# Decay scans ahead of the last attention head, the MLP norm applied to the second product's sums, a 384/128 cut of the last token tile: one change to a one-core decoder block

## The chip, the cores and the metric

The kernel runs on one core of one Trainium2 chip, as one launch. The metric is the device time of one execution in microseconds (us); the time before is the median of 3 runs. Five engines work side by side, each through its own queue in order: TensorE (PE in the profile, with PEld for its weight loads), VectorE (DVE), ScalarE (ACT), GpSimd (POOL) and SyncE (SP). PE reads SBUF and writes PSUM banks of 128 x 512 float32; DVE and ACT read both; transfers are issued from the queues of SP, ACT and POOL.

## What is computed

One layer of a decoder on 512 tokens of width 1024, all float32. Only what the change touches is shown in full:

```
h   = rmsnorm(x, ln1);  one projection h @ w_in -> GLA q,k,v,r,a | attention q,k,v (3 groups) | 2 gates
o   = gla_mixer(q, k, v, log_sigmoid(a @ w_a2 + b_a) / 16)      # 4 heads, chunks, cumulative decay
oat = dilated attention, 3 groups x 4 heads, merged by their softmax denominators
x   = x + (sigmoid(gA) * (o' @ w_o_gla) + sigmoid(gB) * (oat @ w_o_attn)) @ w_out
h2  = rmsnorm(x, ln2)
x   = x + square(relu(h2 @ w_mlp1)) @ w_mlp2
h3  = rmsnorm(x, ln3)
x   = x + sigmoid(h3 @ w_pg) * (p @ w_pp)
out = rmsnorm(x, ln_f)
```

The norm of a token is one factor r = (mean of squares + eps) ** -0.5. Since r is positive, square(relu(r * z)) is r * r * square(relu(z)), so the factor can be put on the hidden units before the square, or, squared, on the sums of the second product.

## The kernel before

**Products.** Every float32 operand is split into a rounded high part and the rest (hi, lo), and a product is three matmuls (hi hi, hi lo, lo hi). `run` (L234 to L241) writes the matmuls to PE in pieces of 8 and calls `step` after each piece; all of them stand on line L240. Most 1024-wide products are done as quads (`strassen`, L266): a 2 x 2 block scheme with 7 stages of 24 matmuls of 256 columns instead of 8 block products. A bank that is finished is copied out by ACT (L312) and the other half added by DVE (L330, L332).

**Weights.** Units of 128 x 1024 stream in through SP (L189). For quads POOL issues transfers that add a second block onto one that has landed (L198, L209), and DVE makes the remaining sums (L206, L212). ACT makes hi (L226), DVE makes lo (L221), a few units ahead of their use (`fetch`, L215).

**What sets the order.** The order is written out by hand. Beside the products stand generators in a list `side`, and closures in a list `later`. `step` (L168) runs one closure of `later` and, once `pace[0]` columns have been written since, one segment of the first generators of `side`, in turn by two (WAYS = 2). `drain` runs all that is left, with no product between.

**Around the change, in the order of the program.** After the attention's v0 the four heads' weighted sums `pv(h)` (scaled probabilities, transposes on PE at L769, products at L775 to L786, a sum on DVE at L788, split at L337 and L345) and then `decay()` are put into `side`, at a pace of 2560 columns, beside the quads gq, gk and gv0. `decay` makes, for each GLA head, a product (L801), an absolute value and a minimum (L805, L806), an exponential (L811), a logarithm (L814) and a cumulative sum by a scan on DVE (L817, L818). After a `drain` come the products `oa` (L1002: 8 tiles of 12 matmuls of 512 columns) with `gla(0)` and `gla(1)` beside them, whose first segments read the cumulative sums (L836 to L861) and are followed by transposes on PE (L869).

Behind w_out the MLP's first product runs as 8 quads (`quad(q)`, L1158 on). Its norm is made by `rms_gen` beside it: four one-column products (L377), the factor by DVE and POOL (L364, L365), a diagonal matrix (L390), its split, and two products that spread the factor over all partitions (L396, L397). Each finished bank is multiplied by it (`scale`, L1167) and squared by ACT (L1176). After the first quad there is a `drain` if the norm isn't there. The second product (L1200 on) sums over 32 hidden units into 4 banks, twice; DVE adds the banks to x (L1226) and `normed` prepares the last norm's operand (L339, L347, L1089).

At the end the gate product `pg` runs per tile of 128 tokens. Per tile: a sigmoid (L1267), a product (L1268), an addition (L1269), a square with a row sum (L1270), the factor (L1281, L1282), then the two halves of the output (L1284, L1290) and their transfers (L1285 on ACT's queue, L1292 on SP's). The last tile's second half is cut into two times 256 columns.

Of the kernel before, what the change touches and what calls it, by code (L numbers as in the profile page):

```python
# [13 lines left out]
AF = mybir.ActivationFunctionType  # L14
# [112 lines left out]
C_LN2, C_LN3, C_BA, C_GN, C_LN1, C_LO, C_N = 0, 8, 16, 20, 28, 36, 38  # L127
W0, W12 = 384, 256

NU, NW, PIECE, WAYS = 69, 5, 8, 2  # L130

NRAW = 6

NWARM = 8

# [2 lines left out]
def block_kernel(ctx, tc, xT, ws, pT, wts, wha, wa2, vec, lnf, rel, onehot, ident_d, mask_d, out):  # L138
# [141 lines left out]
    def halves(t):  # L280
        return slice(t * HT, (t + 1) * HT)
# [88 lines left out]
        S.activation(t, x, AF.Square, scale=1.0 / 32.0)  # L370
        return t

    def rms_tok(acc):

        ps = smt()
        for i in range(4):
            TE.matmul(ps[:, i:i + 1], lhsT=acc[:, i * P:(i + 1) * P], rhs=ones[:, 0:1], start=True, stop=True)  # L377
        r = const.tile([P, 4], F32, name="rtok", bufs=3)
        rsqrt(r, ps[:, 0:4], 4)
        return r  # L380

    def rms_gen(acc, res, wait=0, gap=0):

        for _ in range(wait):
            yield
        r = rms_tok(acc[0])
        for _ in range(gap):
            yield
        dg = u32()
        V.tensor_tensor(dg.rearrange("p (a b) -> p a b", a=4), ident[:, None, :].to_broadcast([P, 4, P]),  # L390
                        r[:, :, None].to_broadcast([P, 4, P]), op=OP.mult)
        dh, dl = split(dg)
        for _ in range(2 + gap):
# [593 lines left out]
    side.append(weights())  # L987
    v0 = values("v0")
    drain()
    pace[0] = 2560  # L990
    side.extend(pv(h) for h in range(4))
    side.append(decay())
    gq = heads("gq", HD_SCALE)
    gk = heads("gk", 1.0)
    gv = [values("gv0", True)]
# [152 lines left out]
        later.extend(x1_tile(j))  # L1148
    while len(later) > 5:
        step()  # L1150
    side.append(rms_gen(acc1, norm2, 6, 2))


    hid = [None] * 32
# [4 lines left out]
    def quad(q):  # L1159


        def finish(m, t, s, ps):
            add(m, s, s, ps)

            def scale():
                o = s.rearrange("p (n t) -> p n t", n=2)
                V.scalar_tensor_tensor(out=o, in0=o, scalar=0.0,  # L1167
                                       in1=norm2[1][:, None, halves(t)].to_broadcast([P, 2, HT]),
                                       op0=OP.max, op1=OP.mult)

            def act():
                for n in range(2):
                    j = 4 * q + 2 * n + m
                    if hid[j] is None:
                        hid[j] = u32()
                    S.activation(hid[j][:, halves(t)], s[:, halves(n)], AF.Square)  # L1176

            later.extend([scale, act])

        def extra(i):  # L1180
            if i in (3, 4):
                later.append(lambda: hid_split(i - 3))

        strassen(f"m1q{q}", x1_op, finish, extra=extra if q == 7 else None)
# [6 lines left out]

    for q in range(8):
        quad(q)
        if q == 0 and not norm2:
            drain()
    for k in (2, 3):
        hid_split(k)
    drain()
# [2 lines left out]
    for sub in range(2):  # L1201
# [21 lines left out]
                    lnb.append(t)  # L1223
        for o in range(4):
            j = 4 * sub + o
            V.tensor_tensor(xx[j], xx[j], pss[o], op=OP.add)  # L1226
            normed(j, C_LN3, x2s, acc2)
    while later:
        step()
# [30 lines left out]
    sp2 = const.tile([P, 4], F32, name="sp2")  # L1260
    fr = const.tile([P, 4], F32, name="fr")

    def gated(ps, i, c, tt, col):

        n = c.stop - c.start
        sg = u32()
        S.activation(sg[:, 0:n], ps[:, 0:n], AF.Sigmoid, scale=rt3[0][:, tt:tt + 1])  # L1267
        V.tensor_tensor(sg[:, 0:n], sg[:, 0:n], pps[i][:, c], op=OP.mult)  # L1268
        V.tensor_tensor(x2t[i][:, c], x2t[i][:, c], sg[:, 0:n], op=OP.add)  # L1269
        S.activation(sg[:, 0:n], x2t[i][:, c], AF.Square, scale=1.0 / 32.0, accum_out=ss2[:, col:col + 1])  # L1270

    def evac_pg0(tt, ps):
        if len(x2t) < 8:
            drain()
        gated(ps, tt, slice(0, 512), tt, tt)
        V.tensor_scalar(sp2[:, tt:tt + 1], ss2[:, tt:tt + 1], EPS, None, op0=OP.add)
        V.tensor_tensor(x2t[tt], x2t[tt], lnb[0], op=OP.mult)

    def scale_out(tt, col):
# [2 lines left out]
        GP.tensor_tensor(fr[:, tt:tt + 1], sp2[:, tt:tt + 1], mh[:, 0:1], op=OP.pow)  # L1282
        o = u32()
        S.activation(o, x2t[tt], AF.Copy, scale=fr[:, tt:tt + 1])  # L1284
        S.dma_start(out[tt * P:(tt + 1) * P, 0:512], o)  # L1285

    def put(tt, c):
        n = c.stop - c.start
# [3 lines left out]
        SY.dma_start(out[tt * P:(tt + 1) * P, 512 + c.start:512 + c.stop], o[:, 0:n])  # L1292

    def evac_pg1(tt, ps):
        gated(ps, 4 + tt, slice(0, 512), tt, 4 + tt)
        scale_out(tt, 4 + tt)
        put(tt, slice(0, 512))

    tmaj("pg0", x2s, evac_pg0)
    tmaj("pg1", x2s, evac_pg1, tts=range(3))  # L1300
    tok = slice(3 * P, 4 * P)
    for f in range(2):
        c = slice(f * 256, (f + 1) * 256)
# [94 lines left out]
```

## Time and profile before

| | us |
|---|---|
| median of 3 runs | 990.1 (989.91 to 991.78) |
| the profiled execution | 991.5 |
| its span (first to last instruction) | 989.7 |
| PE busy in the span | 973.7 |
| DVE, ACT, POOL busy in the span | 689.4, 520.9, 94.4 |

The profiled execution is 1.8 us longer than its span and 1.4 us above the median. Busy time of PE is the union of overlapping matmuls; a product that streams in a row is read by the distance from start to start, not by its own length.

### The profile page before, as it was taken

What the parts mean: (1) busy time and instruction counts of PE and PEld (TensorE: products, weight loads), DVE (VectorE), ACT (ScalarE), POOL (GpSimd) and SP (SyncE); (2) the same over time, 40 slices, a digit from 0 to 9 for tenths busy, and PEclk for the clock granted to TensorE, in tenths of its full rate; (3) what the DMA queues carried; (4) which work ended last, traced back from release to release, by engine and by line L of the source; (5) the groups of instructions that cost most, each with busy time, mean ns of one, the idle gap of its engine ahead of it and who ended that gap; (6) DMA issues with size and microseconds to landing.
All of it is one profiled execution on the core that took longest, in us unless ns stands there. A gap on an engine that the chain in (4) does not pass through costs nothing.

```text
span 989.7 us, 15873 instructions
## 1 busy us (share of the span) xinstructions
PE 973.7 (98%) x6372; PEld 889.3 (90%) x6372; DVE 689.4 (70%) x966; ACT 520.9 (53%) x875; POOL 94.4 (10%) x136
## 2 busy tenths in 40 slices
PE   9999999999998999999999999999999999999996
PEld 7788999999996999999988889999998888888885
DVE  7777579676579669977955697788778445653554
ACT  7335546445575667565733446555665335442633
POOL 0230011320010021013010001010000000000000
PEclk9999999999999999999999999999999999999999
DMA  8473564974264545455636426656544332523102
GB/s 308 126 205 100 128 147 112 266 202 115 80 157 131 160 98 149 121 146 171 171 92 206 126 46 164 177 131 169 154 145 131 104 96 77 167 88 106 43 1 85
DMA packets 40026, 133.63 MB, mean 135 GB/s; under 512 B 5203, under 2 KB 6815, under 8 KB 39952
## 3 DMA queue, kind: packets, MB, share of 16 engines
q1 hardware_dynamic: 27504, 92.51, 28.5%
q0 software_dynamic: 10720, 36.96, 18.4%
q10 hardware_dynamic: 1728, 3.15, 0.8%
q8 instruction: 50, 0.82, 0.3%
q14 instruction: 24, 0.20, 0.1%
HBM read 126.26 MB, written 8.17 MB: 136 GB/s over the span
## 4 chain that ended last, share of the span: by engine, by line
PE 92%; DVE 3%; issue 2%; ACT 1%; POOL 0%; POOLq 0%; DVEq 0%; ACTq 0%
PE mmt L240 73%; PE smt L240 9%; PE smt L829 1%; DVE lo L221 1%; PE smt L769 1%; PE smt L695 1%; PE mmt L454 1%; PE mmt L453 1%; PE mmt L455 1%; PE smt L875 1%; DVE u L818 0%; PE smt L877 0%; PE smt L428 0%; PE smt L665 0%; PE smt L786 0%
## 5 line engine op out<-in xcount | busy, mean ns | idle before, releaser
L240 PE MATMUL mmt<-ur,hi 128*128 128x256 f32 (+1 forms) x2784 | 608.5, 314 | 1.8 <-ACT u L1002 1.5
L240 PEld LDWEIGHTS mmt<-ur,hi 128*128 128x128 f32 x2784 | 459.9, 191 | 34.3 <-issue 1.9
L240 PE MATMUL mmt<-ur,lo 128*128 128x256 f32 (+1 forms) x1392 | 437.4, 314 | 0.5 <-DVE lo L221 0.5
L221 DVE TENSOR_TENSOR lo<-w,hi 128x1024 fp32r<-128x1024 f32 x236 | 286.2, 1220 | 119.6 <-PE mmt L240 64.2
L226 ACT ACTIVATE hi<-w 128x1024 fp32r<-128x1024 f32 x236 | 246.8, 1053 | 137.1 <-issue 64.0
L240 PEld LDWEIGHTS mmt<-ur,lo 128*128 128x128 f32 x1392 | 266.0, 191 | 16.3 <-DVE lo L221 0.7
L240 PE MATMUL mmt<-hi,ur 128*128 128x256 f32 (+1 forms) x736 | 154.5, 306 | 0.0
L337 ACT ACTIVATE ur<-u 128x512 fp32r<-128x512 f32 x136 | 79.9, 621 | 95.2 <-DVE u L1066 30.9
L240 PEld LDWEIGHTS mmt<-hi,ur 128*128 128x128 f32 x736 | 119.4, 191 | 5.6
L240 PE MATMUL mmt<-lo,ur 128*128 128x256 f32 (+1 forms) x368 | 112.4, 305 | 0.0
L345 DVE TENSOR_TENSOR ur<-u,ur 128x512 fp32r<-128x512 f32 x135 | 89.0, 686 | 20.3 <-ACT ur L337 19.7
L330 DVE TENSOR_TENSOR u<-u,mmt 128x512 f32<-128x512 f32 (+1 forms) x92 | 58.0, 654 | 39.0 <-PE mmt L240 37.4
L240 PE MATMUL smt<-ur,hi 128*128 128x512 f32 x272 | 83.7, 389 | 0.0
L312 ACT ACTIVATE u<-mmt 128x512 f32<-128x512 f32 x92 | 54.4, 592 | 49.7 <-PE mmt L240 49.7
L240 PEld LDWEIGHTS mmt<-lo,ur 128*128 128x128 f32 x368 | 70.2, 191 | 2.7
L240 PEld LDWEIGHTS smt<-ur,hi 128*128 128x128 f32 x272 | 51.1, 188 | 10.6
L240 PE MATMUL smt<-ur,lo 128*128 128x512 f32 x136 | 53.0, 390 | 0.0
L209 POOL DMA_DIRECT2D w<-in_wts_dram x23 | 20.1, 875 | 289.8 <-DVE w L206 210.5
L1176 ACT ACTIVATE u<-u 128x256 f32<-128x256 f32 x64 | 23.0, 409 | 37.2 <-DVE u L1167 37.2
L198 POOL DMA_DIRECT2D w<-in_wts_dram x23 | 20.4, 886 | 202.4 <-DMA w<-in_wts_dram 84.6
L240 PEld LDWEIGHTS smt<-ur,lo 128*128 128x128 f32 x136 | 25.5, 188 | 5.3
L212 DVE TENSOR_TENSOR w<-w 128x1024 f32<-128x1024 f32 x23 | 28.2, 1225 | 0.8
(203 smaller groups left out, 718.2 us busy)
## 6 DMA issues: line engine op xcount, KB each, us to landing
w<-in_wts_dram SPq DMA_DIRECT2D x167, 512.0 KB, 4.0
w<-in_wts_dram POOLq DMA_DIRECT2D x46, 512.0 KB, 5.5
u<-in_xT_dram SPq DMA_DIRECT2D x8, 256.0 KB, 4.7
v_dram<-u POOLq DMA_DIRECT2D x8, 256.0 KB, 6.2
u<-v_dram POOLq DMA_DIRECT2D x8, 256.0 KB, 7.3
y_dram<-u ACTq DMA_DIRECT2D x8, 256.0 KB, 2.4
u<-y_dram POOLq DMA_DIRECT2D x8, 256.0 KB, 7.3
u<-in_xT_dram POOLq DMA_DIRECT2D x8, 256.0 KB, 8.1
```

Of the source, the lines that this page charges most:

```text
L198: GP.dma_start(w, wts[UNIT[f"{q}.A22"]], accum_op=OP.add)
L209: GP.dma_start(w, wts[UNIT[f"{q}.A21"]], accum_op=OP.add)
L212: V.tensor_tensor(w, w, raw[f"{q}.A12"], op=OP.add)
L221: V.tensor_tensor(lo, w, hi.bitcast(F32), op=OP.subtract)
L226: S.activation(hi, w, AF.Copy)
L240: TE.matmul(o, lhsT=l, rhs=r, start=a, stop=b, skip_group_check=shared)
L312: S.activation(sums[c], bank[b], AF.Copy, scale=-scale if c[0] else scale)
L330: V.tensor_tensor(out, s, ps, op=OP.subtract if m else OP.add)
L337: S.activation(hi, x, AF.Copy)
L345: V.tensor_tensor(lo, x, hi.bitcast(F32), op=OP.subtract)
L453: TE.matmul(q0ps[i], lhsT=hi[:, c], rhs=xh, start=k == 0, stop=False)
L1176: S.activation(hid[j][:, halves(t)], s[:, halves(n)], AF.Square)
```

## The change

Five edits. (1) `decay` stands ahead of `pv(3)` in the list, and the pace of that stretch stays at 2048 columns instead of 2560. (2) The MLP's norm is made as the square of the factor, by a reciprocal on DVE instead of a power on POOL, starts 30 steps later (6 before), with gaps of 4 steps (2 before); the hidden units are only clipped at zero, and the factor is applied where the second product's banks are added to x, by one more DVE operation for each of the 8 banks. The `drain` after the first quad is gone. (3) The last tile's second half is cut 384 + 128 columns, and the order of its steps is changed: the second sigmoid stands ahead of the first square. (4) Of the first output halves, those of tiles 0 to 2 leave by SP's queue, that of tile 3 by ACT's. (5) The arena has 73 tiles instead of 69, and the space for the descriptors of POOL's transfers is 8192 bytes of each partition instead of 16384.

```diff
-NU, NW, PIECE, WAYS = 69, 5, 8, 2
+NU, NW, PIECE, WAYS = 73, 5, 8, 2
+LAST = 384
...
-    def rms_tok(acc):
+    def rms_tok(acc, squared=False):
...
-        rsqrt(r, ps[:, 0:4], 4)
+        if squared:
+            V.tensor_scalar(r, ps[:, 0:4], EPS, None, op0=OP.add)
+            V.reciprocal(r, r)
+        else:
+            rsqrt(r, ps[:, 0:4], 4)
...
-    pace[0] = 2560
-    side.extend(pv(h) for h in range(4))
-    side.append(decay())
+    side.extend([pv(0), pv(1), pv(2), decay(), pv(3)])
...
-    side.append(rms_gen(acc1, norm2, 6, 2))
+    side.append(rms_gen(acc1, norm2, 30, 4, True))
...
-            def scale():
-                o = s.rearrange("p (n t) -> p n t", n=2)
-                V.scalar_tensor_tensor(out=o, in0=o, scalar=0.0,
-                                       in1=norm2[1][:, None, halves(t)].to_broadcast([P, 2, HT]),
-                                       op0=OP.max, op1=OP.mult)
+            def positive():
+                V.tensor_scalar(s, s, 0.0, None, op0=OP.max)
...
-        if q == 0 and not norm2:
-            drain()
...
-            V.tensor_tensor(xx[j], xx[j], pss[o], op=OP.add)
+            t = u32()
+            V.tensor_tensor(t, pss[o], norm2[1], op=OP.mult)
+            V.tensor_tensor(xx[j], xx[j], t, op=OP.add)
...
-        S.dma_start(out[tt * P:(tt + 1) * P, 0:512], o)
+        (S if tt == 3 else SY).dma_start(out[tt * P:(tt + 1) * P, 0:512], o)
...
-    for f in range(2):
-        c = slice(f * 256, (f + 1) * 256)
-        ps = mmt()
...
-        gated(ps, 7, c, 3, 8 + f)
-        if f == 0:
-            V.tensor_scalar(sp2[:, 3:4], ss2[:, 8:9], sp2[:, 3:4], None, op0=OP.add)
+    parts, sgs = [slice(0, LAST), slice(LAST, 512)], []
+    for c in parts:
+        ps, n = mmt(), c.stop - c.start
...
+        sgs.append(gate(ps, n, 3))
+        if c.start == 0:
+            gated(sgs[0], 7, c)
+    squares(sgs[0], 7, parts[0], 8)
+    gated(sgs[1], 7, parts[1])
+    V.tensor_scalar(sp2[:, 3:4], ss2[:, 8:9], sp2[:, 3:4], None, op0=OP.add)
+    squares(sgs[1], 7, parts[1], 9)
...
-    nc = _bacc.Bacc("TRN2", target_bir_lowering=False, num_devices=1)
+    nc = _bacc.Bacc("TRN2", target_bir_lowering=False, num_devices=1, dynamic_dma_scratch_size=8192)
```

How the order moves, at three places. (The changed kernel has other line numbers: L817 and L818 of before are L823 and L824, L221 is L223, L330 is L332, L345 is L347. Numbers behind a name are buffers.)

DVE at the end of gv0 and the start of `oa`, before: scans (L817, L818) stand among the last sums of gv0 (L330) and directly ahead of the first segment of `gla` (L837).

```order
L818 SCALAR_TENSOR_TENSOR u_3035<-u_135,u_3036 128x512
L345 TENSOR_TENSOR ur_3276<-u_3182,ur_3264 128x512
L817 TENSOR_TENSOR u_3080<-u_3080,u_3079 128x512
L818 SCALAR_TENSOR_TENSOR u_3079<-u_135,u_3080 128x512
L330 TENSOR_TENSOR u_3109<-u_3109,mmt_3011 128x512
L817 TENSOR_TENSOR u_3112<-u_3112,u_3111 128x512
L818 SCALAR_TENSOR_TENSOR u_3111<-u_135,u_3112 128x512
L330 TENSOR_TENSOR u_3146<-u_3146,mmt_3011 128x512
L345 TENSOR_TENSOR ur_3288<-u_3109,ur_3284 128x512
L345 TENSOR_TENSOR ur_3290<-u_3146,ur_3286 128x512
L221 TENSOR_TENSOR lo_3294<-w_3171,hi_3241 128x1024
L837 TENSOR_TENSOR u_3308<-u_3003 128x4x64
```

The same place now, from the last of the four scans (L824) on; the first segment of `gla` follows two rows behind the piece.

```order
L824 SCALAR_TENSOR_TENSOR u_2860<-u_135,u_2861 128x512
L223 TENSOR_TENSOR lo_3179<-w_2788,hi_3147 128x1024
L223 TENSOR_TENSOR lo_3212<-w_3108,hi_3181 128x1024
L332 TENSOR_TENSOR u_3081<-u_3081,mmt_3185 128x512
L347 TENSOR_TENSOR ur_3245<-u_3081,ur_3235 128x512
L223 TENSOR_TENSOR lo_3247<-w_3149,hi_3214 128x1024
L332 TENSOR_TENSOR u_3194<-u_3194,mmt_3072 128x512
L347 TENSOR_TENSOR ur_3280<-u_3194,ur_3270 128x512
L332 TENSOR_TENSOR u_3119<-u_3119,mmt_3013 128x512
L332 TENSOR_TENSOR u_3159<-u_3159,mmt_3013 128x512
L347 TENSOR_TENSOR ur_3288<-u_3119,ur_3284 128x512
L347 TENSOR_TENSOR ur_3290<-u_3159,ur_3286 128x512
```

What moved: the last scans stood among the last sums of gv0 (L330); now all four stand ahead of the last four of these sums (L332), and between the last scan and `gla` there are only sums, splits and weight parts. On PE the last product of `pv(3)` now stands 144 matmuls of 256 columns ahead of the first matmul of `oa`.

DVE in the MLP's first quads, where the norm's factor is made, before (rv and rtok are the factor, u<-ident,rtok the diagonal matrix, rstd the factor on all partitions):

```order
L345 TENSOR_TENSOR ur_6456<-u_6372,ur_6444 128x512
L221 TENSOR_TENSOR lo_6458<-w_6323,hi_6422 128x1024
L364 TENSOR_SCALAR rv_6481<-smt_6475 128x4
L390 TENSOR_TENSOR u_6500<-ident_116,rtok_6480 128x512
L345 TENSOR_TENSOR ur_6504<-u_6500,ur_6502 128x512
L221 TENSOR_TENSOR lo_6506<-w_5928,hi_6460 128x1024
L221 TENSOR_TENSOR lo_6536<-w_6134,hi_6508 128x1024
L221 TENSOR_TENSOR lo_6577<-w_6462,hi_6538 128x1024
L330 TENSOR_TENSOR u_6434<-u_6434,mmt_6545 128x512
L1167 SCALAR_TENSOR_TENSOR u_6434<-u_6434,rstd_6559 128x512
```

The same work now, a quad later:

```order
L1170 TENSOR_SCALAR u_6503<-u_6503 128x512
L223 TENSOR_TENSOR lo_6696<-w_6597,hi_6661 128x1024
L223 TENSOR_TENSOR lo_6731<-w_6228,hi_6698 128x1024
L382 TENSOR_SCALAR rtok_6750<-smt_6745 128x4
L383 RECIPROCAL rtok_6750<-rtok_6750 128x4
L223 TENSOR_TENSOR lo_6769<-w_6462,hi_6733 128x1024
L396 TENSOR_TENSOR u_6797<-ident_116,rtok_6750 128x512
L347 TENSOR_TENSOR ur_6801<-u_6797,ur_6799 128x512
L223 TENSOR_TENSOR lo_6811<-w_6700,hi_6771 128x1024
L332 TENSOR_TENSOR u_6673<-u_6673,mmt_6778 128x512
L1170 TENSOR_SCALAR u_6673<-u_6673 128x512
```

What moved: factor, matrix and split have weight parts between them, and no longer stand ahead of the first hidden sum. On PE, 48 matmuls stood between the one-column products (L377) and the spreading products (L396) before, 6 of them behind the place of L364; now 80.

ACT's last instructions, before (L1267 sigmoid, L1270 square, L1284 output half):

```order
L1284 ACTIVATE u_10052<-u_9680,fr_9779 128x512
L1285 DMA out_0_dram<-u_10052 128x512
L1267 ACTIVATE u_10083<-mmt_10058,rtok_9733 128x256
L1270 ACTIVATE u_10083,ss2_9777<-u_9815 128x256
L1267 ACTIVATE u_10114<-mmt_10089,rtok_9733 128x256
L1270 ACTIVATE u_10114,ss2_9777<-u_9815 128x256
L1284 ACTIVATE u_10121<-u_9696,fr_9779 128x512
L1285 DMA out_0_dram<-u_10121 128x512
```

And now (L1266 sigmoid, L1277 square, L1296 output half, L1297 its transfer):

```order
L1296 ACTIVATE u_10067<-u_9695,fr_9794 128x512
L1266 ACTIVATE u_10098<-mmt_10073,rtok_9748 128x384
L1266 ACTIVATE u_10127<-mmt_10102,rtok_9748 128x128
L1277 ACTIVATE u_10098,ss2_9792<-u_9830 128x384
L1277 ACTIVATE u_10127,ss2_9792<-u_9830 128x128
L1296 ACTIVATE u_10136<-u_9711,fr_9794 128x512
L1297 DMA out_0_dram<-u_10136 128x512
```

What moved: tile 2's transfer is no longer ahead of the last tile's first sigmoid, and the second sigmoid has passed the first square.

## Rows read from the trace of the kernel before

**Rows 1.** Part 1 of the page: each engine's busy time, its share of the span, its instructions.

```profile
PE 973.7 (98%) x6372; PEld 889.3 (90%) x6372; DVE 689.4 (70%) x966; ACT 520.9 (53%) x875; POOL 94.4 (10%) x136
```

**Rows 2.** What PE waited for, over the whole span: us in total, times, the longest.

```profile
PE smt L869 <- DVE u L857: 2.4, 2, 1.6
PE smt L396 <- ACT ur L337: 1.6, 1, 1.6
PE mmt L240 <- ACT u L1002: 1.5, 1, 1.5
PE mmt L240 <- DVE lo L221: 0.5, 1, 0.5
```

**Rows 3.** PE in order of time in the products `oa` with `gla(0)` and `gla(1)` beside them: start, us, instruction, count, idle time before it and what ended it.

```profile
303.20 0.39 PE L240 MATMUL mmt<-ur,lo 128*128 128x512 f32 x1
...
303.88 0.39 PE L240 MATMUL mmt<-ur,lo 128*128 128x512 f32 x1
304.60 0.70 PE L240 MATMUL mmt<-ur,hi 128*128 128x512 f32 x2 [0.32 <-DVE u L330]
...
312.80 0.55 PE L869 MATMUL smt<-ident,u 128*128 128x128 f32 x3 [1.62 <-DVE u L857]
313.10 0.47 PE L240 MATMUL mmt<-ur,lo 128*128 128x512 f32 x1
...
315.09 0.55 PE L869 MATMUL smt<-ident,u 128*128 128x128 f32 x3 [0.82 <-DVE u L857]
315.39 0.71 PE L240 MATMUL mmt<-ur,hi 128*128 128x512 f32 x2
```

**Rows 4.** DVE in order of time in the same stretch: the first and the last scan, the first operation of `gla`, the last one that the second group of transposes (L869) needs.

```profile
295.92 1.23 DVE L818 TENSOR_TENSOR_SCAN u<-u 128x512 f32<-128x512 f32 x1
...
302.64 1.22 DVE L818 TENSOR_TENSOR_SCAN u<-u 128x512 f32<-128x512 f32 x1
...
306.89 0.42 DVE L837 TENSOR_TENSOR u<-u 128x256 f32<-128x256 f32 x1
...
314.75 0.29 DVE L857 COPY u<-u 128x256 f32<-128x256 f32 x1
```

**Rows 5.** Busy time of PE, PEld, DVE, ACT and POOL in the stretch of gq, gk and gv0, with the counts of instructions, the granted clock, the DMA share and GB/s.

```profile
216.00:296.00 80.00, 80.00 (x675) 79.48 (x675) 55.38 (x91) 46.77 (x70) 4.26 (x5) 1.00 0.49 125
```

**Rows 6.** PE in order of time at the end of the MLP's first quad.

```profile
594.27 0.40 PE L240 MATMUL mmt<-ur,hi 128*128 128x256 f32 x2
596.24 0.50 PE L396 MATMUL smt<-ur,ones_r 128*128 128x512 f32 x1 [1.56 <-ACT ur L337]
...
597.55 0.41 PE L240 MATMUL mmt<-ur,lo 128*128 128x256 f32 x1
...
600.33 0.44 PE L240 MATMUL mmt<-ur,hi 128*128 128x256 f32 x2
600.60 0.28 PE L240 MATMUL mmt<-ur,lo 128*128 128x256 f32 x1
...
600.96 0.28 PE L240 MATMUL mmt<-ur,lo 128*128 128x256 f32 x1
```

**Rows 7.** The columns of rows 5, for the stretch of rows 3 and for the one behind L397; behind POOL stands the granted clock, 1.00 for 2.4 GHz and 0.50 for 1.2 GHz.

```profile
304.00:316.00 12.00, 7.75 (x35) 5.38 (x34) 11.34 (x26) 9.80 (x19) 1.06 (x2) 1.00 0.48 154
...
597.50:600.40 2.90, 2.90 (x15) 2.84 (x14) 2.81 (x3) 2.90 (x5) 0.00 (x0) 0.50 0.98 212
```

**Rows 8.** POOL at the same place: the power that makes the norm's factor.

```profile
593.70 1.04 POOL L365 TENSOR_TENSOR rtok<-rv,mh 128x4 f32<-128x4 f32 x1 [14.05 <-DVE rv L364]
```

**Rows 9.** ACT in order of time over the last two tiles (ACTq: issue of a transfer on ACT's queue).

```profile
979.36 0.72 ACT L1284 ACTIVATE u<-u,fr 128x512 f32<-128x512 f32 x1 [0.90 <-POOL fr L1282]
980.11 0.37 ACTq L1285 DMA_DIRECT2D out_dram<-u  x1
980.53 0.47 ACT L1267 ACTIVATE u<-mmt,rtok 128x256 f32<-128x256 f32 x1 [0.45 <-ACT u L1284]
...
982.37 0.46 ACT L1267 ACTIVATE u<-mmt,rtok 128x256 f32<-128x256 f32 x1
983.77 0.42 ACT L1270 ACTIVATE u<-u 128x256 f32<-128x256 f32 x1 [0.95 <-DVE u L1269]
...
985.18 0.72 ACT L1284 ACTIVATE u<-u,fr 128x512 f32<-128x512 f32 x1 [0.90 <-POOL fr L1282]
```

**Rows 10.** DVE at the same place, for the last tile's first 256 columns.

```profile
981.03 0.43 DVE L1268 TENSOR_TENSOR u<-u 128x256 f32<-128x256 f32 x1 [0.92 <-ACT u L1267]
981.50 0.42 DVE L1269 TENSOR_TENSOR u<-u 128x256 f32<-128x256 f32 x1
```

**Rows 11.** PE at the same place: the last long matmul with the first of the last tile, and the last of all.

```profile
975.13 0.51 PE L240 MATMUL mmt<-hi,ur 128*128 128x512 f32 x2
...
981.00 0.28 PE L240 MATMUL mmt<-hi,ur 128*128 128x256 f32 x1
```

**Rows 12.** PE ahead of the gate product: the one-column products of the last norm (each with its own 128 x 128 weights).

```profile
931.74 0.95 PE L377 MATMUL smt<-ones,u 128*128 128x1 f32 x8
```

**Rows 13.** DVE behind the second product: the four banks added to x, and the last of the sums of squares that L377 reads.

```profile
919.86 2.73 DVE L1226 TENSOR_TENSOR u<-u,smt 128x512 f32<-128x512 f32 x4 [7.56 <-PE smt L240]
...
926.96 0.68 DVE L1089 TENSOR_TENSOR u<-u 128x512 f32<-128x512 f32 x1
```

**Rows 14.** Part 3 of the page: POOL's queue, its packets, MB, share of 16 engines.

```profile
q0 software_dynamic: 10720, 36.96, 18.4%
```

More of the change, by code (lines that the diff above doesn't have):

```diff
@@ L378, in rms_tok, with rms_gen @@
         r = const.tile([P, 4], F32, name="rtok", bufs=3)
-        rsqrt(r, ps[:, 0:4], 4)
+        if squared:
[3 more added lines that the diff above has]
+            rsqrt(r, ps[:, 0:4], 4)
         return r
-    def rms_gen(acc, res, wait=0, gap=0):
+    def rms_gen(acc, res, wait=0, gap=0, squared=False):
         for _ in range(wait):
             yield
-        r = rms_tok(acc[0])
+        r = rms_tok(acc[0], squared)
         for _ in range(gap):
@@ L1176, in act @@
                     S.activation(hid[j][:, halves(t)], s[:, halves(n)], AF.Square)
-            later.extend([scale, act])
+            later.extend([positive, act])
         def extra(i):
@@ L1261, in block_kernel, with gate, gated, squares @@
     fr = const.tile([P, 4], F32, name="fr")
-    def gated(ps, i, c, tt, col):
-        n = c.stop - c.start
+    def gate(ps, n, tt):
         sg = u32()
         S.activation(sg[:, 0:n], ps[:, 0:n], AF.Sigmoid, scale=rt3[0][:, tt:tt + 1])
+        return sg
+    def gated(sg, i, c):
+        n = c.stop - c.start
         V.tensor_tensor(sg[:, 0:n], sg[:, 0:n], pps[i][:, c], op=OP.mult)
         V.tensor_tensor(x2t[i][:, c], x2t[i][:, c], sg[:, 0:n], op=OP.add)
+    def squares(sg, i, c, col):
+        n = c.stop - c.start
         S.activation(sg[:, 0:n], x2t[i][:, c], AF.Square, scale=1.0 / 32.0, accum_out=ss2[:, col:col + 1])
+    def gated_all(ps, i, tt, col):
+        sg = gate(ps, 512, tt)
+        gated(sg, i, slice(0, 512))
+        squares(sg, i, slice(0, 512), col)
     def evac_pg0(tt, ps):
@@ L1274, in evac_pg0 @@
             drain()
-        gated(ps, tt, slice(0, 512), tt, tt)
+        gated_all(ps, tt, tt, tt)
         V.tensor_scalar(sp2[:, tt:tt + 1], ss2[:, tt:tt + 1], EPS, None, op0=OP.add)
@@ L1294, in evac_pg1 @@
     def evac_pg1(tt, ps):
-        gated(ps, 4 + tt, slice(0, 512), tt, 4 + tt)
+        gated_all(ps, 4 + tt, tt, 4 + tt)
         scale_out(tt, 4 + tt)
@@ L1301, in block_kernel @@
     tok = slice(3 * P, 4 * P)
-    for f in range(2):
-        c = slice(f * 256, (f + 1) * 256)
-        ps = mmt()
-        run(three(ps[:, 0:256], [(cols(x2s[k], tok), cols(ready[f"pg1.{k // 2}"], slice((k % 2) * 512 + c.start, (k % 2) * 512 + c.stop)))
-                                 for k in range(KC)]))
-        gated(ps, 7, c, 3, 8 + f)
-        if f == 0:
-            V.tensor_scalar(sp2[:, 3:4], ss2[:, 8:9], sp2[:, 3:4], None, op0=OP.add)
+    parts, sgs = [slice(0, LAST), slice(LAST, 512)], []
+    for c in parts:
+        ps, n = mmt(), c.stop - c.start
+        run(three(ps[:, 0:n], [(cols(x2s[k], tok), cols(ready[f"pg1.{k // 2}"], slice((k % 2) * 512 + c.start, (k % 2) * 512 + c.stop)))
+                               for k in range(KC)]))
+        sgs.append(gate(ps, n, 3))
[5 more added lines that the diff above has]
+    squares(sgs[1], 7, parts[1], 9)
     scale_out(3, 9)
```

## The prediction

> **What bounds the kernel now.** I read the busy times first: PE is busy 98% of its span [rows 1], so the kernel is as long as PE's products plus the places where PE stands. The next view is the list of what PE waited for [rows 2]: the waits lie in two short places and nowhere else between. For each I then read PE in order of time and compare the stretch with the same products at full rate. Full rate is read from start to start: a matmul of 512 columns takes 0.227 (three in 303.20 to 303.88 [rows 3]), one of 256 columns 0.12 (three in 600.60 to 600.96 [rows 6]).
>
> First place, the products `oa`: from 303.88 to 315.39 stand 25 matmuls of 512 columns and 6 transposes, three of which take 0.30 (312.80 to 313.10) [rows 3]. At full rate that is 25 x 0.227 + 0.6 = 6.3; it took 11.5. So 5.2 are lost, though the idle times that the waits name sum to 4.2 only [rows 2, 3]: each restart costs some more. The reader is to see why: DVE does the scans of `decay` from 295.9 to 303.9 and begins `gla` at 306.9 [rows 4], while PE is already in `oa`, where the transposes want what `gla` makes.
>
> Second place, the end of the MLP's first quad: PE starts its last pair of short matmuls at 594.27, then waits for the spreading products' operand until 596.24, and runs at full rate again from 600.33 on [rows 6]. Between stand 15 short and 2 long matmuls, 2.25 at full rate; it took 6.06, so 3.8 are lost. Some 1.2 of this is the clock: after the idle time the granted clock is 0.50 (1.2 GHz) for 2.9 us [rows 7], and 13 short matmuls take 2.78 instead of 1.56 [rows 6]. In `oa`, with 4.2 us of idle time in pieces, it stayed at 1.00 [rows 7].
>
> The third place is the tail behind PE's last product at 981.0 [rows 11], a chain through ACT, DVE and POOL.
>
> **The change part by part.**
>
> *Decay ahead of the last head.* Nothing is added; the segments come sooner. gq, gk and gv0 have 63 pieces of 2048 columns (three quads, 7 stages of 3 pieces); heads and decay have 53 segments. At 2560 columns a segment only 50 fit, and the scans were left for the end; at 2048 all 53 are through 10 pieces, 9.6 us, before `oa`. The four scans and the subtractions ahead of them (L817, L818) are 4 x (0.6 + 1.2) = 7.3 of DVE, from start to start [rows 4]; this leaves the stretch behind 295.9, where it was in PE's way. Where does `gla` start then? Behind the last product of `pv(3)`, 144 x 0.12 = 17.3 us ahead of `oa`, DVE has some 21 us of work in the new order: scans 7.3, six weight parts of 1.15, nine sums and splits of 0.6, one sum of 1.1. So `gla` starts some 3.4 us behind the start of `oa` (near 295.9), at 299.3, or at 300.5 with a few waits, instead of 306.9. The second group of transposes needs the copy at 314.75, which ends 8.15 behind the start of `gla` [rows 4]: 308.7. PE, without its waits, gets there 60 long matmuls and three transposes behind 295.9, at 309.8. The margin is 1.1 us, so I take the whole 5.2 as gained; the bounds are 5.5 (an excess also at the neighbours) and 2.6 (half of it stays). Late next on PE there is nothing: the products behind the transposes have no wait in rows 2.
> What hides the denser segments: over gq, gk and gv0 DVE is busy 55.4 of 80 us and PE never idles [rows 5]. About 8 us more makes 63 of 80. I count nothing for it, and up to 1 us for a burst in which a weight part comes late, as it does once now (0.5) [rows 2].
>
> *The norm at the second product's banks.* The same one-column and spreading products stay. The power on POOL (1.04 [rows 8]) goes, a reciprocal of 4 columns on DVE takes its place. What counts is the distance: before, the factor's steps stood 6 matmuls, 0.7 us, ahead of the products that need them; now 80 matmuls, 9.6 us, lie between the one-column products and the spreading ones, for a chain that took 3.5 from the factor's sum to the second spreading product [rows 6, 8]. Nothing reads the factor before the end of the second product's first half, more than 200 us later. I take the whole 3.8; the bounds are 3.0 (some wait with the full clock kept) and 4.0. The clip at zero reads one operand instead of two and is no slower than what it replaces: nothing on PE's path.
> Added are 8 DVE operations. Behind the second half, the four additions end near 922.5 and the sums of squares at 927.6 [rows 13]; with four more operations of 0.6 DVE is some 2.3 later. PE's one-column products that read these sums start at 931.74 [rows 12], so 4.2 us of cover become 1.9: the cost is nothing. If the cover were gone, PE would wait for the rest.
>
> *The tail.* ACT's issue of a transfer (0.37) stood between tile 2's output and the last tile's first sigmoid at 980.53 [rows 9]; it goes to SP, whose queue has nothing else to do, so this sigmoid can start at 980.1. PE's part changes: it starts at 975.36 [rows 11], the 384-column matmuls take 24 x 0.174 (between 0.12 and 0.227), to 979.5. For matmuls of 128 columns there is no row with these operands. The nearest is the single-column product, each with its own weights: 8 in 0.81, so 0.10 [rows 12]; the bounds are 0.06 (half of 256 columns) and 0.12 (no cheaper at all). With 0.10 PE ends at 982.0, 0.8 later than before (981.1), and the second sigmoid starts near 982.2. The steps from sigmoid to product to addition to square are 0.50, 0.47 and 0.45 for 256 columns [rows 9, 10]; for 384 they are 0.6 or so and end at 981.9, ahead of the second sigmoid; for 128 I estimate 0.4, 0.35, 0.35. So the last square starts at 983.3 instead of 983.77, and the 1.41 from there to the last output operation [rows 9] shrink by 0.1: 0.6 gained. With 0.06 a matmul it is 1.2, with 0.12 it is 0.1.
> The Trainium skill (TensorE: Matmul & The Clock Gate, Back-to-back issue gap) gives an isolated matmul 262 cycles at 256 columns and 134 at 128, that is 56 ns. By this the narrow part would take 1.3 us and the tail would gain 1.2; the single-column row, which never falls under 0.10, speaks for a floor by the weights instead.
>
> *Arena and descriptor space.* Four tiles more only make waits for a free tile rarer, and rows 2 name none. Half the descriptor space costs nothing as long as POOL's transfers fit: the queue has 10720 packets in the whole kernel [rows 14], 670 for each of 16 engines.
> The Trainium skill (SBUF — State Buffer, SBUF size: 192, 224, or 256?) names 16 KiB of a partition as the ring of these descriptors, and DMA: Bandwidth & Descriptors (Terms) 16 bytes for each. By these, half of it holds 512 for an engine, most of what the whole kernel uses; the rule would make a rival only if a full ring stopped POOL.
>
> **Sum.** 5.2 + 3.8 + 0.6 = 9.6. The profiled execution took 991.5 (span 989.7); it would take 981.9. The median of the runs is 1.4 below the profiled execution, so the forecast is 990.1 - 9.6 = 980.5.
>
> **The rivals.**
> *The wait of `oa` stays in part* or moves to gv0: DVE is later than my count by more than the 1.1 of margin. For: the margin is small, and scans and weight parts now share one stretch. Against: PE had no wait in 216 to 296 though DVE was busy 55 of 80 [rows 5]. With 2 to 4 us of the 5.2 left: 982.5 to 984.5, say 983.5.
> *The narrow matmuls are cheap* (0.06): the tail gains 0.6 more, 979.9.
> *The norm's price comes at the end of the second product*: DVE is later than the 1.9 of cover left [rows 12, 13], PE stands there for 1 to 2 us and pays the low clock again as in rows 7 (1.2): 983.
> *Slower than before*: half the descriptor space stops POOL. The place is its queue, from which 23 quads take their second blocks; a stop that delays each quad by x costs PE 23 x, and from x = 0.42 on this is more than the 9.6 gained. At 0.6 a quad: 980.5 + 13.8 = 994.3. Against it stands the packet count [rows 14].
>
> **How the numbers follow.** Chances: forecast 0.74, wait of `oa` 0.12, cheap narrow matmuls 0.08, norm at the end 0.03, POOL stopped 0.03. The range goes down to 979.2 (5.5 + 4.0 + 1.2 = 10.7, all upper bounds at once, gives 979.4) and up to 984.0, which takes in most of the wait of `oa`. Measurements of this kernel tell 0.2% (2 us) from no change. All cases but the last lie below 988.1; of the last, half is inside 0.2% and half above, and I add one in a hundred to each for what I don't see: faster 0.95, same 0.025, slower 0.025.
>
> **What would show it.** Right: in the list of PE's waits the lines of L869, L1002 and of the spreading products are gone; the granted clock is 1.00 from 580 to 610; DVE does the scans ahead of `oa`; the last square starts 0.5 sooner behind PE's first matmul of the last tile. Wrong: a wait for DVE's weight parts in gv0, a wait at the last norm's one-column products, POOL transfers that take longer to issue.

## The result, and the profile after

| | before | after |
|---|---|---|
| median of 4 runs, us | 990.9 (989.91 to 994.52) | 983.3 (982.67 to 983.60) |
| the profiled execution | 991.5 | 983.5 |
| its span | 989.7 | 981.7 |

The ratio of the runs is 0.9916, with an interval of 0.9889 to 0.9942: faster by 0.84%. The forecast was 980.5, its range 979.2 to 984.0. The spans differ by 8.0; the forecast's sum was 9.6.

What PE waited for after the change (the view of [rows 2]):

```profile
PE smt L434 <- POOL ones L429: 1.0, 1, 1.0
PE mmt L242 <- DVE lo L223: 0.8, 2, 0.5
PE mmt L460 <- DVE ur L349: 0.3, 1, 0.3
PE mmt L459 <- ACT ur L341: 0.2, 1, 0.2
```

The waits for `gla` and for the spreading products are gone. The first line stands in the trace of before too (1.0, at the program's start). The last two are waits for the first input tiles. But the wait for weight parts (lo) has grown from 0.5 to 0.8, and stands at two places instead of one.

The products `oa` (to set beside [rows 3, 4]): the first of them in the trace of before, then PE and DVE after the change, in order of time: start, duration, instruction, count.

```profile
295.92 0.63 PE L240 MATMUL mmt<-ur,hi 128*128 128x512 f32 x2
```
```profile
296.59 0.63 PE L242 MATMUL mmt<-ur,hi 128*128 128x512 f32 x2
...
309.31 0.49 PE L875 MATMUL smt<-ident,u 128*128 128x128 f32 x3
309.56 0.48 PE L242 MATMUL mmt<-ur,lo 128*128 128x512 f32 x1
...
310.57 0.49 PE L875 MATMUL smt<-ident,u 128*128 128x128 f32 x3
```
```profile
289.71 1.23 DVE L824 TENSOR_TENSOR_SCAN u<-u 128x512 f32<-128x512 f32 x1
...
301.94 0.42 DVE L843 TENSOR_TENSOR u<-u 128x256 f32<-128x256 f32 x1
...
309.45 0.29 DVE L863 COPY u<-u 128x256 f32<-128x256 f32 x1
```

PE goes from the first product of `oa` to the first transposes in 12.72, which is 56 matmuls at the full 0.227. To the second transposes it takes 13.98, where it took 315.09 - 295.92 = 19.17 before: 5.2 gained. The last scan ends at 290.9 instead of 303.9. `gla` starts 5.35 behind the start of `oa`, later than forecast (3.4 to 4.6). The copy that the second transposes need ends at 309.74, and they start at 310.57: the margin is 0.8, where 1.1 was forecast.

The MLP's first quad (to set beside [rows 6, 7]): PE at the two late weight parts, DVE's parts that end the waits, and the windows of `oa` and of this place with the columns of [rows 5].

```profile
581.55 0.40 PE L242 MATMUL mmt<-ur,hi 128*128 128x256 f32 x2
582.47 0.39 PE L242 MATMUL mmt<-ur,lo 128*128 128x256 f32 x1 [0.52 <-DVE lo L223]
...
588.31 0.40 PE L242 MATMUL mmt<-ur,hi 128*128 128x256 f32 x2
589.01 0.39 PE L242 MATMUL mmt<-ur,lo 128*128 128x256 f32 x1 [0.30 <-DVE lo L223]
```
```profile
581.19 1.22 DVE L223 TENSOR_TENSOR lo<-w,hi 128x1024 fp32r<-128x1024 f32 x1
...
587.73 4.63 DVE L223 TENSOR_TENSOR lo<-w,hi 128x1024 fp32r<-128x1024 f32 x4
```
```profile
304.00:316.00 12.00, 12.00 (x63) 9.78 (x62) 11.15 (x23) 8.71 (x19) 1.90 (x3) 1.00 0.55 193
580.00:610.00 30.00, 29.18 (x240) 28.59 (x239) 26.32 (x33) 20.72 (x32) 2.58 (x3) 1.00 0.64 167
```

The granted clock is 1.00 in both stretches. The second wait costs 0.46 from start to start (0.70 between the two rows, less two matmuls of 0.12). In the kernel before, the eight one-column products of the norm stood on PE between the same two places, and took 0.81 from their first start to the next product's. PE and DVE there:

```profile
587.87 0.95 PE L377 MATMUL smt<-ones,u 128*128 128x1 f32 x8
...
593.79 0.28 PE L240 MATMUL mmt<-ur,lo 128*128 128x256 f32 x1
```
```profile
592.32 1.22 DVE L221 TENSOR_TENSOR lo<-w,hi 128x1024 fp32r<-128x1024 f32 x1
```

PE came to the second place at 593.79, when DVE's part had been done since 593.54: it did not wait.

The last norm (to set beside [rows 12, 13]): the last sum of squares on DVE, and the products on PE that read it.

```profile
922.05 0.69 DVE L1093 TENSOR_TENSOR u<-u 128x512 f32<-128x512 f32 x1
```
```profile
924.16 0.95 PE L379 MATMUL smt<-ones,u 128*128 128x1 f32 x8
```

The cover is 1.4, down from 4.1; the forecast left 1.9 of it. PE does not wait.

The tail (to set beside [rows 9, 11]): PE, then ACT.

```profile
967.55 0.56 PE L242 MATMUL mmt<-hi,ur 128*128 128x512 f32 x2
967.95 0.34 PE L242 MATMUL mmt<-lo,ur 128*128 128x384 f32 x1
...
972.03 0.27 PE L242 MATMUL mmt<-lo,ur 128*128 128x128 f32 x1
...
974.48 0.28 PE L242 MATMUL mmt<-hi,ur 128*128 128x128 f32 x1
```
```profile
972.40 0.56 ACT L1266 ACTIVATE u<-mmt,rtok 128x384 f32<-128x384 f32 x1
974.79 0.37 ACT L1266 ACTIVATE u<-mmt,rtok 128x128 f32<-128x128 f32 x1 [1.83 <-PE mmt L242]
...
975.85 0.31 ACT L1277 ACTIVATE u<-u 128x128 f32<-128x128 f32 x1 [0.18 <-DVE u L1273]
...
977.15 0.72 ACT L1296 ACTIVATE u<-u,fr 128x512 f32<-128x512 f32 x1 [0.90 <-POOL fr L1294]
```

The last tile's first matmul starts at 967.78 (the second of the x2). From there to ACT's last output operation it is 9.37; before it was 985.18 - 975.36 = 9.82. So 0.45 is gained. The last square (975.85) starts 8.07 behind that first matmul, where it was 8.41: 0.34 sooner, 0.5 was forecast. The second sigmoid waits 1.83 for PE: the narrow products, 0.111 apart (22 distances in 972.03 to 974.48), end last.

The span's balance: `oa` starts 0.7 later (296.59 against 295.92), 0.6 of it from the first 10 us; `oa` itself gains 5.2. For 580 to 600, what each start-to-start distance on PE has over the full rate adds up to 4.6 before and 1.6 now, so 3.0 are gained there, and 0.45 in the tail. Sum 5.2 + 3.0 + 0.45 - 0.7 = 7.95, against 8.0.

### The profile page after: what moved, and what is told of

It is laid out like the page before. It is cut to its first block, busy times and chain, and to the rows that moved or that the text cites. A ratio compares the mean times of both kernels' runs of the same rounds, so it can differ in the third digit from the quotient of the medians.

```text
span 981.7 us, 15874 instructions
## 1 busy us (share of the span) xinstructions
PE 972.4 (99%) x6372; PEld 889.3 (91%) x6372; DVE 686.0 (70%) x975; ACT 523.1 (53%) x875; POOL 94.3 (10%) x135
## 4 chain that ended last, share of the span: by engine, by line
PE 96%; DVE 2%; issue 1%; DMA 1%; ACT 0%; SPq 0%; POOLq 0%; POOL 0%; DVEq 0%
PE mmt L242 77%; PE smt L242 9%; PE smt L835 1%; PE smt L775 1%; PE smt L701 1%; PE smt L881 1%; PE mmt L460 1%; DMA u<-in_xT_dram 1%; PE mmt L461 0%; DVE lo L223 0%; PE mmt L459 0%; PE smt L883 0%; DVE ur L347 0%; PE smt L792 0%; PE smt L671 0%
## 5 line engine op out<-in xcount | busy, mean ns | idle before, releaser
L223 DVE TENSOR_TENSOR lo<-w,hi 128x1024 fp32r<-128x1024 f32 x236 | 286.8, 1221 | 115.3 <-PE mmt L242 68.8
L242 PE MATMUL mmt<-hi,ur 128*128 128x256 f32 (+3 forms) x736 | 155.6, 307 | 0.0
L242 PE MATMUL mmt<-lo,ur 128*128 128x256 f32 (+3 forms) x368 | 113.1, 307 | 0.0
L347 DVE TENSOR_TENSOR ur<-u,ur 128x512 fp32r<-128x512 f32 x135 | 89.0, 687 | 19.6 <-ACT ur L339 19.1
L332 DVE TENSOR_TENSOR u<-u,mmt 128x512 f32<-128x512 f32 (+1 forms) x92 | 57.8, 655 | 34.3 <-PE mmt L242 34.0
```

The lines of the kernel that those rows point to most:

```text
L223: V.tensor_tensor(lo, w, hi.bitcast(F32), op=OP.subtract)
L242: TE.matmul(o, lhsT=l, rhs=r, start=a, stop=b, skip_group_check=shared)
L332: V.tensor_tensor(out, s, ps, op=OP.subtract if m else OP.add)
L347: V.tensor_tensor(lo, x, hi.bitcast(F32), op=OP.subtract)
```

## The experiments

Each trace is compared at the place that its edit touches. The time of the kernel before has a wide spread, so the time of each kernel stands with its ratio to before and the interval. Times also hold what the start of the program does: in the traces `oa` begins at 296.59 in the changed kernel and between 295.45 and 296.43 in the others, without an edit ahead of it that adds to or takes from PE's work. So a difference of about 1 us or less between two kernels is read from the place in the trace and not from the times.

**One part alone.** Four kernels, each the kernel before with one part of the change.

```diff
only_decay:
-    pace[0] = 2560
-    side.extend(pv(h) for h in range(4))
-    side.append(decay())
+    side.extend([pv(0), pv(1), pv(2), decay(), pv(3)])
only_norm:
-    side.append(rms_gen(acc1, norm2, 6, 2))
+    side.append(rms_gen(acc1, norm2, 30, 4, True))
...
+            V.tensor_tensor(t, pss[o], norm2[1], op=OP.mult)
only_tail:
+LAST = 384
...
-        S.dma_start(out[tt * P:(tt + 1) * P, 0:512], o)
+        (S if tt == 3 else SY).dma_start(out[tt * P:(tt + 1) * P, 0:512], o)
only_space:
-NU, NW, PIECE, WAYS = 69, 5, 8, 2
+NU, NW, PIECE, WAYS = 73, 5, 8, 2
...
+    nc = _bacc.Bacc("TRN2", target_bir_lowering=False, num_devices=1, dynamic_dma_scratch_size=8192)
```

> The kernel before with the decay edit alone (decay ahead of pv(3), pace 2048 in that stretch). Theory: the products oa lost 5.2 us before because DVE scanned until 303.9; the edit alone takes 5.0 to 5.3 out of the trace, PE waits at L869 and for L1002 are gone, the waits at the MLP's first quad (L396 1.6, lo 0.5) stay: 985.0 or so against 990.1, ratio 0.995. Rival: the gain of the whole change in oa needs the four arena tiles more, since the denser segments hold more tiles at once: then PE shows waits in 216 to 303 and the gain is 3 or less, 987 or more.

Measured: 987.4, ratio 0.9958 (0.9945 to 0.9972). `oa` has no wait, as expected. But by the medians only 3.8 are gained, and PE has a new wait in its list:

```profile
PE smt L829 <- DVE ur L908: 1.1, 1, 1.1
```

Followed back, ACT and then DVE in order of time:

```profile
427.17 0.42 ACT L905 ACTIVATE ur<-u 128x256 fp32r<-128x256 f32 x1 [4.35 <-PE smt L829]
427.49 1.04 ACT L226 ACTIVATE hi<-w 128x1024 fp32r<-128x1024 f32 x1
```
```profile
428.57 1.23 DVE L221 TENSOR_TENSOR lo<-w,hi 128x1024 fp32r<-128x1024 f32 x1 [3.76 <-ACT hi L226]
...
430.97 1.09 DVE L908 TENSOR_TENSOR ur<-u,ur 128x256 fp32r<-128x256 f32 x3
```

ACT stands 4.35 at a split of `gla`, released by a PE product that does not make its input: this looks like a wait for the tile that it writes. Behind it on ACT is a weight's hi part, DVE waits for that, and PE for DVE. So 5.2 are gained in `oa`, and 1.1, with the restart 1.3, given back. The kernel before had the same ACT wait, hidden from PE (line L905: what its engine waited for):

```profile
  PE smt L829: 3.8, 1
```

In the changed kernel, with its four tiles more, this wait is gone from ACT too.

> The kernel before with the norm edit alone (square of the factor, later start, factor at the second product's banks, no drain). Theory: 3.0 gained net and not the 3.8 of the forecast: the 3.8 between 594 and 600 goes, and PE's wait for a weight part (lo) at two places of the first quad comes to 1.2 in all instead of 0.7, because the eight one-column products no longer stand ahead of the second place. 987.1, ratio 0.997. Rival: the second late weight part comes from the four arena tiles or the decay edit, and is missing here: 3.8 gained, 986.3, one wait for lo only.

Measured: 988.6, ratio 0.9977 (0.9966 to 0.9987). PE waits twice for lo, as in the whole change, so the second late part is the norm edit's own:

```profile
PE mmt L240 <- DVE lo L221: 0.8, 2, 0.5
```

In 580 to 600 the trace lost 1.6, 3.0 less than the profiled execution of before. The 3.0 is as expected, and the rival, with one wait for lo only, is out.

> The kernel before with the tail edits alone (384 + 128 columns, second sigmoid ahead of the first square, three output transfers by SP). Theory: from PE's first matmul of the last tile to the last output operation on ACT 9.37 instead of 9.82, so 0.45 gained, 989.7; not to be told from no change in the times, only in the trace. Rival: the transfers on SP's queue are what gains; then the first sigmoid of the last tile is what ends last, and the matmuls of 128 columns cost nothing: 9.0.

Measured: 990.8, ratio 0.9990 (0.9980 to 1.0000). The time tells little, as expected. In the trace the tail, from the last tile's first matmul (973.38) to ACT's last output operation, takes 9.37. PE, then ACT:

```profile
973.15 0.56 PE L242 MATMUL mmt<-hi,ur 128*128 128x512 f32 x2
```
```profile
982.75 0.72 ACT L1297 ACTIVATE u<-u,fr 128x512 f32<-128x512 f32 x1 [0.90 <-POOL fr L1295]
```

That is the value of the whole change, so the tail edits do the same by themselves; the 9.0 of the rival didn't come.

> The kernel before with 73 arena tiles and half the descriptor space alone. Theory: no change, within 0.1% of the kernel before, the same waits of PE, and the issue of POOL's 46 transfers of weights takes as long as before (0.88 each). Rival: the smaller ring stops POOL at some quads, seen as longer issues; or the added tiles take waits away: a change of 0.5 us or more either way.

Measured: 990.9, ratio 0.9993 (0.9984 to 1.0003). POOL's issues take 0.88 as before. By themselves, tiles and descriptor space together do nothing that can be measured. The trace shows something else, though. The place of [rows 6] is there with almost the same idle time (1.49 and 0.22 instead of 1.56 and 0.23), but not the low clock of [rows 7]:

```profile
597.50:600.40 2.90, 2.90 (x27) 2.90 (x26) 2.90 (x4) 2.90 (x5) 0.00 (x0) 1.00 0.98 205
```

27 matmuls in these 2.9 us against 15. PE lost 2.3 in the ten us from 590 on, against 3.7 in the execution of before that the forecast was read from. The trace of only_tail, with this place untouched and 1.56 and 0.23 of idle time as in before, has 2.3 too, that of only_decay (1.57 and 0.22) has the low clock and 3.8. From only_tail, PE at the wait and the window behind it:

```profile
595.74 0.49 PE L398 MATMUL smt<-ur,ones_r 128*128 128x512 f32 x1 [1.56 <-ACT ur L339]
```
```profile
596.80:599.70 2.90, 2.90 (x26) 2.89 (x25) 2.90 (x3) 2.90 (x5) 0.00 (x0) 1.00 0.97 184
```

So the low clock behind this wait comes in some executions and not in others. Of 53 executions of the kernel before that ran beside the experiments, 26 have a mean granted clock of 0.997 or 0.998 and a median of 990.3, and 27 one of 0.995 or 0.996 and 992.2; the median of all is 991.6. That fits, but these executions have no trace, and the two groups are 1.9 apart where the low clock explains 1.4.

**Order or pace.** Two kernels, the changed one with one half of the decay edit undone.

```diff
pace_2560:
+    pace[0] = 2560
     side.extend([pv(0), pv(1), pv(2), decay(), pv(3)])
decay_last:
-    side.extend([pv(0), pv(1), pv(2), decay(), pv(3)])
+    side.extend([pv(0), pv(1), pv(2), pv(3), decay()])
```

> The changed kernel with the pace of 2560 columns put back, decay still ahead of pv(3): the order alone. Theory: what gains in oa is that all segments are through before oa, and this is the pace's doing; at 2560 the last scans stand again two sums and a weight part ahead of gla, so 3 to 5 us of the 5.1 come back: 986.5 to 988.5, with PE waiting at L875 and for L1006. Rival: the order does it; then 983.3 or so and no such wait.

> The changed kernel with decay behind pv(3) again, at the pace of 2048 columns: the pace alone. Theory: the scans are through 10 pieces ahead of oa in this order too, so the trace has no wait in oa and the time is that of the changed kernel, 983.3 within 0.5. Rival: the order is needed; some scans or the sums of pv(3) are late and PE waits 1 to 5 us between 296 and 316: 984.5 to 988.

Measured: pace_2560 988.7, ratio 0.9967 (0.9956 to 0.9978), and PE waits in `oa` again; 4.4 of the 5.2 come back in the trace:

```profile
PE smt L875 <- DVE u L863: 2.5, 2, 2.0
PE mmt L242 <- ACT u L1007: 1.2, 1, 1.2
```

decay_last 982.9, ratio 0.9914 (0.9895 to 0.9933), without a wait in `oa`; from the start of `oa` to PE's last product its trace takes as long as the changed kernel's (677.9). So the pace does all of it. The order, after which the edit is named, does nothing at this pace, and at most 0.8 at the old one.

**The tiles, with the rest of the change.**

```diff
-NU, NW, PIECE, WAYS = 73, 5, 8, 2
+NU, NW, PIECE, WAYS = 69, 5, 8, 2
```

> The changed kernel with 69 arena tiles. Theory: the wait of 1.1 that the decay edit alone showed in the second quad of GLA work (PE for L908 of DVE, behind an ACT split that stood 4.35 for a tile) is a wait for a free tile, and comes back: 984.4, PE waits 1.1 at the line of the GLA products. Rival: another part of the change moved that place, the tiles do nothing: 983.3 and no such wait.

Measured: 984.3 (984.07 to 984.40), ratio 0.9927 (0.9911 to 0.9943). The wait is back:

```profile
PE smt L835 <- DVE ur L914: 1.1, 1, 1.1
```

So it is a wait for a free tile, as the rival of only_decay had it, though at another place, and the four tiles are worth 1.0 by the times and 1.3 in the trace (the wait and its restart) once the pace is changed. Alone they were worth nothing.

**The place of the norm's products.**

```diff
-    side.append(rms_gen(acc1, norm2, 30, 4, True))
+    side.append(rms_gen(acc1, norm2, 6, 4, True))
```

> The changed kernel with the MLP norm's products after 6 steps as before, with the gaps of 4. Theory: the one-column products stand again ahead of the second place where PE waited for a weight part (0.30 idle, 0.46 lost in all) and cover it; the spreading products come 51 matmuls, 6.1 us, behind them, while DVE is full, and may wait up to 1.5: 982.9 without such a wait, 984.5 with all of it. Rival: the late weight part has nothing to do with the place of these products: two waits for lo stay, 983.3 or more.

Measured: 982.3 (981.97 to 982.75), ratio 0.9907 (0.9891 to 0.9924). PE in order of time, and DVE's next late part:

```profile
581.77 0.39 PE L242 MATMUL mmt<-ur,lo 128*128 128x256 f32 x1 [0.53 <-DVE lo L223]
...
593.07 0.39 PE L402 MATMUL smt<-ur,ones_r 128*128 128x512 f32 x1
```
```profile
587.03 1.22 DVE L223 TENSOR_TENSOR lo<-w,hi 128x1024 fp32r<-128x1024 f32 x1
```

The one-column products, at 582.59, cover the second late part, and PE waits for lo once. The spreading products at 593.07, 10.5 later, do not wait. From 580 to 600 the trace loses 0.9 instead of 1.6, so 0.7 is gained. The distance that the norm needs is the gap behind its one-column products; the later start gained nothing here and took their cover away.

**DVE's work ahead of the weight parts.** The last two additions of the norm's squares are made later.

```diff
+            if j > 5:
+                tail.append(sq)
-            if j:
+            elif j:
...
+        for sq in tail:
+            V.tensor_tensor(acc1[0], acc1[0], sq, op=OP.add)
+            yield
```

> The changed kernel with the last two of the eight additions that gather the MLP norm's squares moved behind the first stages of the first quad (they stand now ahead of its weight parts on DVE). Theory: in 577 to 592 DVE is never idle and PE's two waits for lo (0.52 and 0.30 idle, 1.3 lost in all with the restarts) are DVE's work; with 0.6 to 1.2 less ahead of them the first wait is 0.1 or gone and the second gone: 1.0 to 1.3 gained, 982.1. Rival: these waits hang on the transfers or on ACT's hi parts: both stay, 983.3.

Measured: 982.2 (981.99 to 982.52), ratio 0.9909 (0.9893 to 0.9926). The time is the expected one by luck: half of the expectation fell. The first wait is gone, the second (0.3) stays, and in 580 to 600 the trace gains 0.7 of the 1.0 to 1.3; `oa` began 0.3 sooner. DVE at the two places:

```profile
580.25 1.22 DVE L223 TENSOR_TENSOR lo<-w,hi 128x1024 fp32r<-128x1024 f32 x1
...
586.79 4.62 DVE L223 TENSOR_TENSOR lo<-w,hi 128x1024 fp32r<-128x1024 f32 x4
```

From the one lo to the other it is 6.54 here and 6.54 in the changed kernel: the edit moved both PE and DVE forward and left DVE's work between the two places as it was. So the first wait is set by DVE's work ahead of it. That the second is set by the work between the two fits, and was not tested by itself.

**The cut of the last tile.**

```diff
-LAST = 384
+LAST = 256
```

The other kernel has 320 there.

> The changed kernel with the last tile's second half cut 256 + 256 again, in the new order of steps. Theory: a matmul of 128 columns took 0.112, of 256 columns 0.12 and of 384 0.173, so the narrow cut costs PE 24 x (0.173 + 0.112 - 2 x 0.12) = 1.1; with 256 + 256 the second sigmoid starts 1.1 to 1.2 sooner, the steps behind it are 0.35 longer, the last square starts some 0.8 sooner and the tail (first matmul of the last tile to the last output operation on ACT) takes 8.7 instead of 9.37: 982.6. Rival: the shorter steps of the narrow part are worth more than the matmuls: 9.4 or more, 983.3 to 983.8.

> The changed kernel with the last tile's second half cut 320 + 192. Theory, as for 256 + 256, with some 0.147 and 0.115 a matmul: PE takes 0.55 less than with 384 + 128, the steps are 0.18 longer, tail 8.95: 982.9. Rival (short steps are worth more): 9.4 or more.

Measured: 982.4 (982.3 to 982.6), ratio 0.9912 (0.9898 to 0.9927), and 982.35 (981.98 to 982.94), ratio 0.9912 (0.9897 to 0.9927). With 256 + 256, PE and then ACT:

```profile
966.95 0.51 PE L242 MATMUL mmt<-hi,ur 128*128 128x512 f32 x2
```
```profile
973.13 0.47 ACT L1266 ACTIVATE u<-mmt,rtok 128x256 f32<-128x256 f32 x1 [0.87 <-PE mmt L242]
...
975.97 0.72 ACT L1296 ACTIVATE u<-u,fr 128x512 f32<-128x512 f32 x1 [0.91 <-POOL fr L1294]
```

The tail takes 975.97 - 967.18 = 8.79, with 320 + 192 it takes 8.97, with 384 + 128 9.37. The order of the steps, with the transfers on SP, gained 9.82 - 8.79 = 1.03 of the tail; the narrow cut gave 0.58 of this back. How the 1.03 divides between order and transfers was not tested.

**The two that gained, together.**

```diff
-LAST = 384
+LAST = 256
...
-    side.append(rms_gen(acc1, norm2, 30, 4, True))
+    side.append(rms_gen(acc1, norm2, 6, 4, True))
```

> The changed kernel with the norm's products after 6 steps (gaps of 4) and the last tile cut 256 + 256: the two edits that gained by themselves. Theory: they lie in different places and add, 0.72 at the first quad and 0.58 in the tail of the trace: 983.3 - 1.3 = 982.0, or 981.7 from the median of the one less the gain of the other; one wait for lo (0.5) is left, and the tail takes 8.8. Rival: PE that is sooner in one place waits elsewhere, and no more than the better of the two is left: 982.3 or more.

Measured: 981.5 (981.24 to 982.04), ratio 0.9899 (0.9882 to 0.9915). One wait for lo is left (0.5). PE and then ACT in the tail:

```profile
965.89 0.50 PE L242 MATMUL mmt<-hi,ur 128*128 128x512 f32 x2
```
```profile
974.90 0.72 ACT L1296 ACTIVATE u<-u,fr 128x512 f32<-128x512 f32 x1 [0.91 <-POOL fr L1294]
```

ACT's last output operation starts 8.78 behind the last tile's first matmul (966.12, the second of the x2). So both gains stand in one trace, and this kernel has the lowest median of the study.

## Why the prediction was right, and where its sizes were off

Direction and places held. The range held in part by luck: it went up to 984.0 for a wait left over in `oa`, which did not come, and the room was used up by other terms. The forecast was 2.8 too low, by these:

- **`oa`, 5.2 forecast, 5.2 in the trace.** Right, and right that the scans would be through ahead of `oa`; pace_2560 and decay_last put it down to the pace alone. `gla` was later than the working had it (5.35 behind the start of `oa`), but 0.8 of the margin was left.
- **The norm, 3.8 forecast, 3.0 in the trace.** The mis-sized term. The one-column products were counted as staying, and what they hid at their old place was not seen: moved away from 587.87, they leave DVE's second weight part bare. The forecast had "I take the whole 3.8; the bounds are 3.0 (...)", and the lower bound is what came, for another reason.
- **The low clock, 1.2 to 1.4, counted on the wrong basis.** The forecast took 1.4 off the profiled execution's time to come to the median, and still subtracted a loss in which that execution's low clock stood. Two of the three runs shown (990.1, 989.91) were as fast as executions without it. They have no trace; if they were such, their loss from 590 on was 2.3 and not 3.7, as in only_space and only_tail, and this part of the gain wasn't there to take: against the 3.1 that only_space loses in 580 to 600, the norm's gain is 1.5. From spans alone: 8.0 gained; from the median 990.1 to 983.3: 6.8. That the median of three fell among the faster executions was chance: the 53 later ones have a median of 991.6, close to the profiled 991.5.
- **The tail, 0.6 forecast, 0.45 in the trace.** A matmul of 128 columns took 0.111, not 0.10. The nearest row, the one-column product, pointed the right way, and 0.111 lies midway between it and the upper bound of 0.12. That the narrow cut costs more than it saves was not seen. The Trainium skill (TensorE: Matmul & The Clock Gate, Back-to-back issue gap) gives 56 ns for an isolated one and about 81 ns for one in a stream with weight loads; here, with 128 x 128 float32 weights each time, neither holds, and the measured 0.111 decides.
- **Not in the sum:** the first 10 us took 0.6 longer. The waits for the first input tiles come and go in the kernels above, whose first instructions are the same (none in before, only_norm 0.2, only_tail 0.3, last_256 0.7). I put it down to the landing of the first transfers, which no experiment tested.
- **Tiles, counted at nothing.** Wrong as reasoned: [rows 2] lists only PE's waits, and the tile wait stood on ACT, 3.8 long and hidden. The decay edit laid it bare (only_decay, 1.1), and the four tiles took it away (arena_69).
- **Half the descriptor space:** nothing, as forecast, though it was run only together with the tiles. The Trainium skill (SBUF — State Buffer, SBUF size: 192, 224, or 256?) sets 16 KiB of a partition aside for the ring of these descriptors. With half of it POOL's issues took 0.88 as before, and no trace here shows a ring that stops POOL.

Of the rivals none came. `oa` has no wait left. The wait at the end of the second product stayed away, with 1.4 of cover. The cheap narrow matmuls fell with the 0.111.

## What to carry to other kernels

Before subtracting a loss from a median, check that the median's runs have it: a loss that hangs on the clock may stand in the profiled execution and not in them. When a step is moved, ask what it hid at its old place, not only what waits at the new one. Search the waits of all engines, not just of the one that bounds the kernel, for those that are hidden now and bare after the next edit. Narrowing the last piece pays only down to the width below which a product gets no cheaper.

## What the hardware showed that was not expected

After the same idle time (1.56 and 0.23 in before and in only_tail) and in the same instructions, PE's granted clock fell to 0.50 for 2.9 us in the profiled execution of before and stayed at 1.00 in that of only_tail.

Start to start, with 128 x 128 weights of its own, a matmul took 0.111 for 128 columns (the changed kernel), 0.112 for 192 (21 distances in the rows below, from last_320), 0.12 for 256, 0.147 for 320, 0.173 for 384 and 0.227 for 512: straight down to 256, and flat from 192 to 128. PE's rows for 192 columns, the first and the last part of them:

```profile
970.79 0.28 PE L242 MATMUL mmt<-lo,ur 128*128 128x192 f32 x1
...
973.14 0.28 PE L242 MATMUL mmt<-lo,ur 128*128 128x192 f32 x1
```
